# Two-layer diffusion transformer block on one core: modulation sums of the second layer begun two steps sooner, and the last gate multiplied into weights instead of results

## The chip, the cores and the metric

The kernel runs as one launch on one core of a Trainium2 chip. A core has five engines with queues of their own: PE (TensorE, matmuls), DVE (VectorE), ACT (ScalarE), POOL (GpSimd) and SP (SyncE, which here only issues DMAs). Every instruction waits in its engine's queue behind the one ahead of it. The metric is the time of one execution in device microseconds (us), the median of several runs.

## The reference

Two layers over 256 latent tokens and 256 context tokens of width 1024. Each layer modulates its input, mixes (layer 0: retention, layer 1: neighbourhood attention), adds the result through a gate, normalizes, modulates again, runs an MLP of width 4096 and adds that through a second gate. Only the latent rows of layer 1 are returned. What matters here:

```python
def sq_relu_mlp(h, w1, w2):
    return jnp.square(jax.nn.relu(h @ w1)) @ w2
...
    for i in range(DEPTH):
        mod = (silu_c @ ada_w[i] + ada_b[i])[:, None, :]
        mod_c = silu_cc @ ada_w[i] + ada_b[i]
        sh1, sc1, g1, sh2, sc2, g2 = jnp.split(mod, 6, axis=-1)
        ...
        x = layer_norm(DN_ALPHA * x + g1 * y, ln_g[i, 0], ln_b[i, 0])
        h = x * (1.0 + sc2) + sh2
        x = layer_norm(DN_ALPHA * x + g2 * sq_relu_mlp(h, mlp_w1[i], mlp_w2[i]), ln_g[i, 1], ln_b[i, 1])
```

`g2` is one row of 1024 numbers, the same for all tokens, so `g2 * (hidden @ w2)` equals `hidden @ (w2 * g2)`, column by column.

## The kernel before

**Weights.** Every weight is used as a sum of two halves in a rounded 32-bit format, `hi` and `lo`, and each product takes three matmuls (hi*hi, hi*lo, lo*hi). Weights come in *units* of 512 KB: SP loads one into a buffer `raw` (pool `rawp`, four buffers), ACT casts it to `hi`, DVE subtracts to get `lo`, and that subtraction sets the `raw` buffer free. `hi` and `lo` have five buffers each (`WB = 5`), which PE sets free when it is done with a unit. The list `specs` holds the order of the units, `fetch` loads and splits one, `take` hands out the next and keeps five ahead.

**Background stream.** The modulation rows of both layers (`silu(c) @ ada_w`) are not made on PE: `bg_stream` runs in 89 small steps beside other work. A step takes a 512 KB tile `rawa` of `ada_w` (from the same four `rawp` buffers, loaded one step ahead), and DVE weighs it into `acc` (`weigh`: one pass of 128x1024 for latent alone, two passes where the context's modulation is wanted as well). After eight steps `folded` reduces `acc` to `red`; small operations on POOL (columns) or DVE and POOL (`ada_gate`) then finish a row. Steps 1 to 41 are done in the retention stage, and the other 48 belong to layer 1. A call `bg()` does one step, up to `bg_max`.

**First MLP (layer 0, 512 tokens).** The hidden width goes in two halves (`hf`). For each, eight groups `fp` of 256 hidden columns are made (two units, 48 matmuls each), then two output halves, eight units each (24 matmuls per unit). In the very last output half the last four units are *held* and used token tile by token tile, so that the next layer's start overlaps. Before the change the 48 steps run from the output halves of `hf` 0 on: one per unit there (16), then `bg(2 + fp % 2)` in the groups of `hf` 1 (20), one per unit in the third output half (8) and in the first four units of the last (4). Instructions are placed by a scheduler except where an engine is set to program order (`.on = True`); SP is always in program order.

**Second MLP (layer 1, 256 tokens) and the end.** `mm2b(t, half, u, un)` adds unit `u` (16 units of 256 hidden rows by 512 columns, for each `half`) into `parts[t, half]` for the token tile `t`. Units 0 to 12 are used as they come; units 13 to 15 of both halves (`HELD = 13`) are held and used in the order: tile 0 half 0, tile 0 half 1, tile 1 half 0, tile 1 half 1 (this last in two column quarters, in two banks of their own). `settle` multiplies a bank by the gate row `G2` and adds it to the residual rows `R`; `settle_quarter` does it for a quarter; `stat` takes the statistics of the norm, and `last_norm` and the stores end the kernel.

Names in the rows: `p` are the matmul banks, `raw` weights, `rawa` tiles of `ada_w`, `hid` the hidden activations, `r` their relu, `st` statistics, `G` a gate row. Line 84 is the helper through which all operations are issued, so nearly every row has it. The four held units of the first MLP's last output half are called h1 to h4 below; the unit ahead of them U4.

Of the kernel before, what the change touches and what calls it, by code (L numbers as in the profile page):

```python
# [17 lines left out]
P = 128  # L18
# [86 lines left out]
def kernel(  # L105
# [23 lines left out]
    pe, act, dve, pool, sp = (  # L129
        InOrder(tc, getattr(nc, e), e in PIN)  # L130
        for e in ("tensor", "scalar", "vector", "gpsimd", "sync")
    )
# [23 lines left out]
    def bank(s="ps"):  # L156
        return psp.tile([P, 512], F32, tag="ps", name=nm(s))
# [5 lines left out]
    def scr(s, dt=F32):  # L163
        return scp.tile([P, 512], dt, tag="scr", name=nm(s))
# [18 lines left out]
    specs = []  # L183
# [54 lines left out]
    def spec_w2(u, half):  # L238
        w_rows(mlp_w2[1], u * 256, 256, half * 512, 512)


    scratch_units = set()
    for u in range(16):
        for half in range(2):
            if (u, half) == (10, 0):
                scratch_units.add(len(specs))
                spec_w2(13, 0)
            if (u, half) != (13, 0):
                spec_w2(u, half)

    units = []
# [3 lines left out]
    def fetch(n, in_scratch=False, at=None):  # L255

        for src, k, ncol in specs[len(units) : len(units) + max(n, 0)]:
            raw = rawp.tile([P, k, ncol], F32, tag="raw", name=nm("raw"))
            sp.dma_start(out=raw[:], in_=src.rearrange("(k p) n -> p k n", p=P))
            if in_scratch or len(units) in scratch_units:  # L260
                hi, lo = Rows([scr("hi", F32R) for _ in range(k)]), Rows([scr("lo", F32R) for _ in range(k)])
                for i in range(k):
                    act.copy(out=hi[:, i, :], in_=raw[:, i, :])
                    pending.append((lo[:, i, :], raw[:, i, :], hi[:, i, :]))
                units.append((hi, lo))
                continue
            if at is None:
                hi = hip.tile([P, k, ncol], F32R, tag="hi", name=nm("hi"))
                lo = lop.tile([P, k, ncol], F32R, tag="lo", name=nm("lo"))
            else:  # L270
                both = slot(at, [P, 2, k, ncol], F32R, "hilo")
                hi, lo = both[:, 0], both[:, 1]
            act.copy(out=hi[:], in_=raw[:])
            pending.append((lo[:], raw[:], hi[:]))
            units.append((hi, lo))
# [99 lines left out]
    R = [RR[t // 2][:, t % 2, :] for t in range(4)]  # L375
# [180 lines left out]
    def bg(n=1):  # L556
        for _ in range(n):
            if bg_done[0] < bg_max[0]:
                flush()
                bg_done[0] += 1  # L560
                next(bgs, None)
# [5 lines left out]
    def load_gate(l, w, nt=2, eng=nc.scalar):  # L567
        G = cpool.tile([P, 2, D], F32, tag="G", name=nm("G"))
        gt = grow[l, w]
        for t in range(nt):  # L570
            eng.dma_start(out=G[:, t, :], in_=gt[t : t + 1, :].broadcast_to([P, D]))
        return G
# [83 lines left out]
    def stat(t, half):  # L656
        if half == 0:
            stats[t] = smp.tile([P, 2, 6], F32, tag="st", name=nm("st"))
        dve.bn_stats(out=stats[t][:, half, :], in_=R[t][:, half * 512 : (half + 1) * 512])
# [212 lines left out]
    def part_v(k, a, b):  # L872
# [8 lines left out]
        out=lgn[:, 0], in_=ret_decay[0].rearrange("(o d) h -> o (d h)", o=1).broadcast_to([P, 8])  # L881
# [118 lines left out]
    for h in range(RH):  # L1000
# [9 lines left out]
        else:  # L1010
# [15 lines left out]
            for u in range(4):  # L1026
                ((wh, wl),) = take(1)
                for t in range(4):
                    for kk in range(2):
                        k = 2 * u + kk  # L1030
# [72 lines left out]
        for t in range(4):  # L1103
            po = bank("po")
            scs = list(range(4)) if t < 2 else [2, 3]
            for i, sc in enumerate(scs):
# [9 lines left out]
                out=on, in0=po[:], scalar1=mv[:, 0:1], scalar2=r[:], op0=ALU.subtract, op1=ALU.mult  # L1116
# [51 lines left out]
        else:  # L1168
# [35 lines left out]
            tmp = proj(1, 1)  # L1204
# [10 lines left out]
            tmp = proj(2, 1)  # L1215
# [54 lines left out]

    G2 = None
    for hf in range(2):
# [46 lines left out]
        for fp in range(len(hid), 8):  # L1319
            ht = hslot(fp)  # L1320
            pb = [bank("p1") for _ in range(2)]
            us = take(2)
            mm1(us, ALL, pb)
            pe.on = False
            dve.on = hf == 0
            evac1(pb, ALL, ht)
            if hf == 0 and fp < 6:
                residual(fp - 2, xns[fp - 2], gb, dve)
            dve.on = False
            hid.append(ht)  # L1330
            if hf:
                bg(2 + fp % 2)
            if hf == 0 and fp < 6:
                for q in range(16 * (fp - 2), 16 * (fp - 1)):
                    shifted_biases(q)
        if G2 is None:
            G2 = load_gate(0, 1)
        for half in range(2):
# [19 lines left out]
            if not last:  # L1358
                for t in range(4):
                    accumulate(pb[t], t, half, G2)  # L1360
                continue
            bg_until(89)
            held = take(4)
# [14 lines left out]
            def settle(t):  # L1378

                add_to(t, 1, gated(pb[t], t, 1, G2), dve)  # L1380
                stat(t, 1)
                return moments(t)
# [336 lines left out]
    p2 = turn(2)  # L1719
# [183 lines left out]
    ps = bank("pnw")  # L1903
# [93 lines left out]
    ps = [wo_last(1, 1, cols) for cols in HALVES]  # L1997
# [58 lines left out]


    G2 = load_gate(1, 1, 1)
    HS1 = [N_Q, N_V, N_B, N_P0, N_P1, N_OH, N_OL, N_K1]
    hid = [ht]  # L2060
    for f4 in range(1, 8):
# [22 lines left out]

    FULL = slice(0, 512)
    parts = {(t, half): [(bank("p2"), FULL)] for t in range(2) for half in range(2)}
    HELD = 13

    def mm2b(t, half, u, un, only=None):
        wh, wl = un  # L2090
        for i, (ps, cols) in enumerate(parts[t, half]):
            if only in (None, i):
                for kk in range(2):
                    k = 2 * u + kk
                    ht = hid[k // 4]
                    mm3(
                        ps[:, cols],
                        (ht[:, k % 4, 0, tsl(t)], ht[:, k % 4, 1, tsl(t)]),
                        (wh[:, kk, cols], wl[:, kk, cols]),
                        k == 0 or (len(parts[t, half]) > 1 and k == 2 * HELD),  # L2100
                        k == 31 or (t == half == 1 and k == 2 * HELD - 1),
                    )

    held = {}
    for u in range(HELD):
        if u == 10:
# [13 lines left out]
    def quarter(q):  # L2120
        return slice(256 * q, 256 * q + 256)
# [3 lines left out]

    def settle_quarter(q):
        ps = parts[1, q // 2][q % 2][0][:, quarter(q % 2)]
        tmp = scr("acc")
        dve.tensor_mul(out=tmp[:, :256], in0=ps, in1=G2[:, 0, quarter(q)])
        dve.tensor_add(out=R[1][:, quarter(q)], in0=R[1][:, quarter(q)], in1=tmp[:, :256])  # L2130
        stat_quarter(q)

    def stat_quarter(q):
# [14 lines left out]
        if a:  # L2148
            (sp, act)[half].dma_start(out=out[0, tsl(t), sl], in_=xn)

    for half in range(2):
        for u in range(13, 16):
            mm2b(0, half, u, held[u, half])
        if half == 0:
            settle(1, 1)
            parts[1, 1] = [(bank("p2"), slice(256 * q, 256 * q + 256)) for q in range(2)]
        settle(0, half)
        stat(0, half)
    m0 = moments(0)
    for half in range(2):  # L2160
        last_norm(0, 0, half, *m0)
# [51 lines left out]
```

## Time and profile before

| | |
|---|---|
| median of 3 runs | 1175.99 us (1175.35 to 1176.32) |
| the profiled execution | 1176.32 us, span of its instructions 1174.4 us |
| granted TensorE clock | 0.998 of full speed |
| busy: PE, DVE, ACT, POOL | 1161.8, 848.4, 481.1, 235.1 us |
| instructions | 17544 |
| HBM read, written | 189.12 MB, 5.75 MB |

Matmul records overlap each other (a 128x512 matmul is shown with 0.39 us, while the next one starts 0.23 us later), so PE's pace is read from the distance of starts and its waits from larger distances. An `[idle <-X]` at the end of a row is the time that this engine stood idle ahead of the row, and what ended it. A row with xN merges N like operations.

### The profile page before, as it was taken

The page shows a single profiled execution, that of the slowest core. Times are in us where ns is not written, and L with a number is a line of the kernel's source. Part 1 is how long each engine was busy: PE and PEld are TensorE (multiplying, and loading weights), DVE is VectorE, ACT ScalarE, POOL GpSimd, SP SyncE. Part 2 cuts the span into 40 slices and gives each one's busy share as a digit, 9 for nine tenths or more (in the row PEclk, how much of TensorE's full clock was granted, in tenths as well). Part 3 has the DMA queues.
Part 4 walks back from the last instruction along what each step waited for, and adds up shares of the span by engine and source line. Part 5 has one row for each costly group of instructions (what it writes and reads, how often), then busy time and mean ns, then how long its engine had stood idle before and what let it go on. Part 6 is the DMA issues. An engine that isn't in the chain of part 4 may idle for free.

```text
span 1174.4 us, 17544 instructions
## 1 busy us (share of the span) xinstructions
PE 1161.8 (99%) x6687; PEld 980.7 (84%) x6687; DVE 848.4 (72%) x1361; ACT 481.1 (41%) x819; POOL 235.1 (20%) x418
## 2 busy tenths in 40 slices
PE   9999999999999999999999999999999999999997
PEld 6788888888888889888888888879778878999886
DVE  3786687777898787757777675578577589877456
ACT  3643332222323246441212333137466666756341
POOL 0102001010220241770312001223443430000001
PEclk9999999999999999999999999999999999999999
DMA  9943552544355426756556665646344335766760
GB/s 275 277 130 105 162 187 96 156 153 144 112 178 177 140 65 220 181 113 215 177 184 198 211 200 179 197 157 202 81 136 144 107 113 160 214 206 205 237 215 36
DMA packets 140115, 195.10 MB, mean 166 GB/s; under 512 B 9936, under 2 KB 81136, under 8 KB 140032
## 3 DMA queue, kind: packets, MB, share of 16 engines
q1 hardware_dynamic: 131904, 182.03, 49.8%
q0 software_dynamic: 6976, 9.39, 3.8%
q10 hardware_dynamic: 1152, 2.56, 0.7%
q8 instruction: 52, 0.85, 0.3%
q14 instruction: 31, 0.25, 0.1%
HBM read 189.12 MB, written 5.75 MB: 166 GB/s over the span
## 4 chain that ended last, share of the span: by engine, by line
PE 74%; DMA 12%; DVE 8%; issue 3%; ACT 2%; POOL 0%; DVEq 0%; ACTq 0%
PE p L84 23%; DMA rawa<-in_ada_w_dram 11%; PE pq L84 8%; PE pv L84 8%; PE pw L84 7%; PE pg L84 7%; PE pn L84 4%; DVE acc L84 4%; PE pnv L84 4%; PE po L84 3%; DVE lo L84 3%; PE pnw L84 1%; PE ppt L84 1%; PE pS L84 1%; PE pav L84 1%
## 5 line engine op out<-in xcount | busy, mean ns | idle before, releaser
L84 ACT CAST hi<-raw 128x1024 fp32r<-128x1024 f32 (+2 forms) x228 | 231.9, 1032 | 306.7 <-PE p L84 114.2
L84 DVE TENSOR_TENSOR lo<-raw,hi 128x1024 fp32r<-128x1024 f32 (+2 forms) x228 | 272.6, 1210 | 101.3 <-ACT hi L84 101.1
L84 PE MATMUL p<-hi,hid 128*128 128x512 f32 (+1 forms) x780 | 238.2, 386 | 0.0
L84 PEld LDWEIGHTS p<-hi,hid 128*128 128x128 f32 x780 | 145.7, 188 | 29.3
L84 PE MATMUL p<-hTl,hi 128*128 128x256 f32 (+1 forms) x512 | 165.9, 326 | 0.0
L84 PE MATMUL p<-hTh,lo 128*128 128x256 f32 (+1 forms) x512 | 165.9, 326 | 0.0
L84 PE MATMUL p<-hTh,hi 128*128 128x256 f32 (+1 forms) x512 | 162.6, 327 | 0.0
L84 PE MATMUL p<-lo,hid 128*128 128x512 f32 (+1 forms) x390 | 150.8, 387 | 2.1 <-DVE lo L84 2.1
L84 DVE SCALAR_TENSOR_TENSOR acc<-rawa,scol,acc 128x1024 f32<-128x1024 f32 x56 | 74.4, 1341 | 65.1 <-DMA rawa<-in_ada_w_dram 65.1
L84 PEld LDWEIGHTS p<-hTh,lo 128*128 128x128 f32 x512 | 96.3, 188 | 8.8
L84 PEld LDWEIGHTS p<-hTl,hi 128*128 128x128 f32 x512 | 96.4, 188 | 8.7
L84 PEld LDWEIGHTS p<-hTh,hi 128*128 128x128 f32 x512 | 94.3, 188 | 8.7
L84 PEld LDWEIGHTS p<-lo,hid 128*128 128x128 f32 x390 | 73.3, 188 | 17.9 <-DVE lo L84 3.2
L84 DVE SCALAR_TENSOR_TENSOR strips<-rawa,scol,strips 128x512 f32<-128x512 f32 x112 | 78.6, 764 | 0.0
L84 ACT CAST hid<-r 128x256 fp32r<-128x256 f32 (+1 forms) x64 | 31.9, 500 | 112.4 <-DVE r L84 112.3
L84 POOL TENSOR_TENSOR rstd<-rstd,misc 128x1 f32<-128x1 f32 x28 | 19.1, 684 | 216.5 <-DVE rstd L84 215.5
L84 ACT ACTIVATE s<-s,mn 128x512 f32<-128x512 f32 x64 | 45.5, 713 | 21.6 <-DVE mn L84 21.6
L84 PE MATMUL pw<-hi,oh 128*128 128x512 f32 x128 | 50.8, 397 | 0.0
L84 PE MATMUL pg<-hi,hTh 128*128 128x512 f32 x128 | 50.6, 395 | 0.0
L84 PE MATMUL pw<-hi,ol 128*128 128x512 f32 x128 | 50.0, 390 | 0.0
L84 PE MATMUL pg<-hi,hTl 128*128 128x512 f32 x128 | 49.9, 390 | 0.0
L84 PE MATMUL pw<-lo,oh 128*128 128x512 f32 x128 | 49.8, 389 | 0.0
(241 smaller groups left out, 2275.2 us busy)
## 6 DMA issues: line engine op xcount, KB each, us to landing
raw<-in_mlp_w_dram SPq DMA_DIRECT2D x128, 512.0 KB, 4.5
rawa<-in_ada_w_dram SPq DMA_DIRECT2D x80, 512.0 KB, 3.9
raw<-in_ret_w_in_dram SPq DMA_DIRECT2D x42, 512.0 KB, 4.0
raw<-in_nat_w_in_dram SPq DMA_DIRECT2D x24, 512.0 KB, 4.1
rawq<-in_ada_w_dram SPq DMA_DIRECT2D x16, 512.0 KB, 6.0
raw<-in_ret_w_o_dram SPq DMA_DIRECT2D x16, 512.0 KB, 3.5
bias<-rpb_rows POOLq DMA_DIRECT2D x32, 128.0 KB, 2.9
raw<-in_nat_w_o_dram SPq DMA_DIRECT2D x8, 512.0 KB, 3.7
```

What stands on the lines that cost most here:

```text
L84: r = f(*args, **kwargs)
```

## The change

Three things are changed.

1. In the groups `fp` 6 and 7 of the first MLP's first half, one `bg()` each is added. The 48 steps of layer 1 so begin two calls sooner and end two calls sooner; the last two calls, in the units ahead of the held ones, find nothing left to do.
2. The units (13, 1), (14, 1) and (15, 1) of the second MLP's second half are multiplied in place by the gate row on DVE, after their load and before their split.
3. For half 1, the banks of units 0 to 12 are closed at unit 12 for both token tiles (before: only tile 1) and settled through the gate; units 13 to 15 go to new banks, which are added to `R` without a gate.

```diff
+    HELD = 13
+    scratch_units, scaled_units, scale_row = set(), set(), [None]
     for u in range(16):
         for half in range(2):
             ...
             if (u, half) != (13, 0):
+                if half == 1 and u >= HELD:
+                    scaled_units.add(len(specs))
                 spec_w2(u, half)
...
             sp.dma_start(out=raw[:], in_=src.rearrange("(k p) n -> p k n", p=P))
+            if len(units) in scaled_units:
+                dve.tensor_mul(
+                    out=raw[:], in0=raw[:], in1=scale_row[0].unsqueeze(1).broadcast_to([P, k, ncol])
+                )
...
             if hf:
                 bg(2 + fp % 2)
+            elif fp > 5:
+                bg()
...
     G2 = load_gate(1, 1, 1)
+    scale_row[0] = G2[:, 0, 512:1024]
...
-                        k == 0 or (len(parts[t, half]) > 1 and k == 2 * HELD),
-                        k == 31 or (t == half == 1 and k == 2 * HELD - 1),
+                        k == 0 or (half == 1 and k == 2 * HELD),
+                        k == 31 or (half == 1 and k == 2 * HELD - 1),
...
     def settle_quarter(q):
         ps = parts[1, q // 2][q % 2][0][:, quarter(q % 2)]
-        tmp = scr("acc")
-        dve.tensor_mul(out=tmp[:, :256], in0=ps, in1=G2[:, 0, quarter(q)])
-        dve.tensor_add(out=R[1][:, quarter(q)], in0=R[1][:, quarter(q)], in1=tmp[:, :256])
+        dve.tensor_add(out=R[1][:, quarter(q)], in0=R[1][:, quarter(q)], in1=ps)
         stat_quarter(q)
...
-    for half in range(2):
-        for u in range(13, 16):
-            mm2b(0, half, u, held[u, half])
-        if half == 0:
-            settle(1, 1)
-            parts[1, 1] = [(bank("p2"), slice(256 * q, 256 * q + 256)) for q in range(2)]
-        settle(0, half)
-        stat(0, half)
+    for u in range(HELD, 16):
+        mm2b(0, 0, u, held[u, 0])
+    settle(0, 0)
+    stat(0, 0)
+    for t in range(2):
+        settle(t, 1)
+    parts[0, 1] = [(bank("p2"), FULL)]
+    parts[1, 1] = [(bank("p2"), slice(256 * q, 256 * q + 256)) for q in range(2)]
+    for u in range(HELD, 16):
+        mm2b(0, 1, u, held[u, 1])
+    dve.tensor_add(out=R[0][:, FULL.stop :], in0=R[0][:, FULL.stop :], in1=parts[0, 1][0][0][:])
+    stat(0, 1)
```

How instructions move, at three places. First, SP's queue around group `fp` 6 of the first half, before:

```order
L84 DMA raw_4560<-in_mlp_w_dram 128x2x512
L84 DMA raw_4627<-in_mlp_w_dram 128x2x512
L84 DMA raw_4633<-in_mlp_w_dram 128x2x512
L84 DMA raw_4704<-in_mlp_w_dram 128x2x512
L84 DMA raw_4710<-in_mlp_w_dram 128x2x512
L84 DMA rawa_4740<-in_ada_w_dram 128x2x512
L84 DMA raw_4746<-in_mlp_w_dram 128x2x512
L84 DMA rawa_4776<-in_ada_w_dram 128x2x512
L84 DMA raw_4780<-in_mlp_w_dram 128x2x512
```

and with the change:

```order
L84 DMA raw_4560<-in_mlp_w_dram 128x2x512
L84 DMA rawa_4624<-in_ada_w_dram 128x2x512
L84 DMA raw_4633<-in_mlp_w_dram 128x2x512
L84 DMA raw_4639<-in_mlp_w_dram 128x2x512
L84 DMA rawa_4703<-in_ada_w_dram 128x2x512
L84 DMA raw_4714<-in_mlp_w_dram 128x2x512
L84 DMA raw_4720<-in_mlp_w_dram 128x2x512
L84 DMA rawa_4750<-in_ada_w_dram 128x2x512
L84 DMA raw_4754<-in_mlp_w_dram 128x2x512
L84 DMA rawa_4784<-in_ada_w_dram 128x2x512
```

The four weight units that stood ahead of the first of these `rawa` tiles (4627 to 4710) now have two of them (4624, 4703) in between; from there on each weight unit stands behind two more `rawa` tiles than before, until the stream ends. The very first tile of the stream (step 0, `rawa_3389`) is loaded long ahead in both.

Second, DVE's queue at the end of the stream. Before, from step 46's weighing to the second held unit (h1's subtraction writes `lo_6281`, h2's `lo_6314`; `p_929` and `p_930` are banks of the third output half):

```order
L84 SCALAR_TENSOR_TENSOR acc_6161<-rawa_6341,scol,acc_6161 128x1024
L84 TENSOR_TENSOR acc_6268<-p_929_5977,G_4697 128x512
L84 BN_STATS st_6420<-R_104 128x6
L84 TENSOR_TENSOR acc_6271<-p_930_5978,G_4697 128x512
L84 TENSOR_TENSOR lo_6281<-raw_6278,hi_6280 128x1024
L84 BN_STATS st_6422<-R_104 128x6
L84 SCALAR_TENSOR_TENSOR acc_6161<-rawa_6374,scol,acc_6161 128x1024
L84 BN_STATS st_6424<-R_105 128x6
L84 TENSOR_REDUCE red_6160<-acc_6161 128x32
L84 BN_STATS st_6426<-R_105 128x6
L84 COPY gate_6452<-red_6160 64x32
L84 TENSOR_TENSOR lo_6314<-raw_6311,hi_6313 128x1024
```

With the change, from the last step's weighing (h1 is `lo_6287`; behind the last row stand six small gate operations and then `lo_6320`, h2):

```order
L84 SCALAR_TENSOR_TENSOR acc_6101<-rawa_6314,scol,acc_6101 128x1024
L84 TENSOR_REDUCE red_6100<-acc_6101 128x32
L84 TENSOR_TENSOR lo_6238<-raw_6235,hi_6237 128x1024
L84 TENSOR_TENSOR acc_6268<-p_929_5981,G_4707 128x512
L84 TENSOR_TENSOR acc_6271<-p_930_5982,G_4707 128x512
L84 BN_STATS st_6420<-R_104 128x6
L84 TENSOR_TENSOR acc_6274<-p_931_5983,G_4707 128x512
L84 BN_STATS st_6422<-R_104 128x6
L84 BN_STATS st_6424<-R_105 128x6
L84 TENSOR_TENSOR acc_6277<-p_932_5984,G_4707 128x512
L84 TENSOR_TENSOR lo_6287<-raw_6284,hi_6286 128x1024
L84 BN_STATS st_6426<-R_105 128x6
```

The last weighing and its reduction now stand ahead of U4 (`lo_6238`) and of all four settled banks, and no weighing is left between h1 and the others.

Third, DVE's queue over the second MLP's last units. Before, from unit (11, 1) on ((12, 0), (12, 1), (13, 1), (14, 0), (14, 1), (15, 0), (15, 1)):

```order
L84 TENSOR_TENSOR lo_10778<-raw_10775,hi_10777 128x1024
L84 TENSOR_TENSOR lo_10784<-raw_10781,hi_10783 128x1024
L84 TENSOR_TENSOR lo_10802<-raw_10799,hi_10801 128x1024
L84 TENSOR_TENSOR lo_10820<-raw_10817,hi_10819 128x1024
L84 TENSOR_TENSOR lo_10838<-raw_10835,hi_10837 128x1024
L84 TENSOR_TENSOR lo_10856<-raw_10853,hi_10855 128x1024
L84 TENSOR_TENSOR lo_10874<-raw_10871,hi_10873 128x1024
L84 TENSOR_TENSOR lo_10892<-raw_10889,hi_10891 128x1024
```

and with the change:

```order
L84 TENSOR_TENSOR lo_10778<-raw_10775,hi_10777 128x1024
L84 TENSOR_TENSOR raw_10817<-raw_10817,G_9373 128x1024
L84 TENSOR_TENSOR lo_10784<-raw_10781,hi_10783 128x1024
L84 TENSOR_TENSOR lo_10802<-raw_10799,hi_10801 128x1024
L84 TENSOR_TENSOR raw_10854<-raw_10854,G_9373 128x1024
L84 TENSOR_TENSOR lo_10821<-raw_10817,hi_10820 128x1024
L84 TENSOR_TENSOR lo_10839<-raw_10836,hi_10838 128x1024
L84 TENSOR_TENSOR raw_10891<-raw_10891,G_9373 128x1024
L84 TENSOR_TENSOR lo_10858<-raw_10854,hi_10857 128x1024
L84 TENSOR_TENSOR lo_10876<-raw_10873,hi_10875 128x1024
L84 TENSOR_TENSOR lo_10895<-raw_10891,hi_10894 128x1024
```

Each of the three multiplications stands two subtractions ahead of its own unit's, and so in front of subtractions of units that are already loaded. The order of PE's matmuls and of SP's loads is unchanged here.

More of the change, by code (lines that the diff above doesn't have):

```diff
@@ L239, in spec_w2 @@
         w_rows(mlp_w2[1], u * 256, 256, half * 512, 512)
-    scratch_units = set()
+    HELD = 13
+    scratch_units, scaled_units, scale_row = set(), set(), [None]
     for u in range(16):
@@ L2086 @@
     parts = {(t, half): [(bank("p2"), FULL)] for t in range(2) for half in range(2)}
-    HELD = 13
     def mm2b(t, half, u, un, only=None):
```

## The prediction, on record before the changed kernel ran

> **What bounds the kernel now.** I read the page's busy shares first, then the waits, then PE's timeline at the only place where PE waits, then the chain of work through that place.
>
> ```profile
> PE 1161.8 (99%) x6687; PEld 980.7 (84%) x6687; DVE 848.4 (72%) x1361; ACT 481.1 (41%) x819; POOL 235.1 (20%) x418
> PE p L84 <- DVE lo L84: 2.1, 2, 1.7
> ```
>
> PE is busy for 99% of the span, but a modelled matmul overlaps the next one, so the share alone proves little. The second row, from the waits between 760 and 775 us, is the better witness: PE waited there for DVE's `lo` of a weight unit, twice, and its timeline shows what that cost.
>
> ```profile
> 765.02 0.39 PE L84 MATMUL p<-lo,hid 128*128 128x512 f32 x1
> 765.70 0.39 PE L84 MATMUL p<-lo,hid 128*128 128x512 f32 x1
> 768.23 0.50 PE L84 MATMUL p<-lo,hid 128*128 128x512 f32 x1 [1.70 <-DVE lo L84]
> 770.33 0.50 PE L84 MATMUL p<-lo,hid 128*128 128x512 f32 x1 [0.43 <-DVE lo L84]
> 772.52 0.39 PE L84 MATMUL p<-lo,hid 128*128 128x512 f32 x1
> ```
>
> Matmuls with `lo` come once in three, 0.68 us apart at full pace (765.02 to 765.70). Between 765.70 and 772.52 there are six such distances, 4.08 us at pace, and they took 6.82: PE lost **2.74 us** at the held units h1 to h4. Behind the first 60 us I found no other distance of starts far beyond the pace, so nearly everything that is to be gained lies here or behind PE's last matmul. The chain of waits through this place:
>
> ```profile
> 748.30 3.97 DMA rawa<-in_ada_w_dram
> 753.68 3.59 DMA rawa<-in_ada_w_dram
> 759.11 3.90 DMA rawa<-in_ada_w_dram
> 763.10 1.28 DVE acc L84
> 764.91 1.23 DVE red L84
> 766.95 1.23 DVE lo L84
> 769.07 1.22 DVE lo L84
> ```
>
> It is the background stream in lock step: a tile lands after some 3.6 to 4.0 us, DVE weighs it, a buffer comes free, the next tile is asked for. One turn takes about 5.3 us. The weight units' `lo` stand between these in DVE's queue and come as late as the stream does. The three tiles shown are those of steps 45, 46 and 47, the last; 763.10 is step 47's weighing.
>
> **The two steps that begin sooner.** They are two turns of the same lock step, taken out of its end and put into groups 6 and 7 of the first half. There:
>
> ```profile
> 511.75 1.05 ACT L84 CAST hi<-raw 128x1024 fp32r<-128x1024 f32 x1 [0.22 <-PE p L84]
> 515.56 1.23 DVE L84 TENSOR_TENSOR lo<-raw,hi 128x1024 fp32r<-128x1024 f32 x1 [1.50 <-ACT hi L84]
> 518.07 0.69 DVE L84 TENSOR_TENSOR hid<-r,hid 128x512 fp32r<-128x512 f32 x1 [0.69 <-ACT hid L84]
> 522.63 1.05 ACT L84 CAST hi<-raw 128x1024 fp32r<-128x1024 f32 x1 [0.56 <-PE p L84]
> 528.18 1.41 DVE L84 TENSOR_SCALAR acc<-rawa,scol 128x1024 f32<-128x1024 f32 x2
> 530.11 2.47 DVE L84 SCALAR_TENSOR_TENSOR acc<-rawa,scol,acc 128x1024 f32<-128x1024 f32 x2
> 538.85 1.22 DVE L84 TENSOR_TENSOR lo<-raw,hi 128x1024 fp32r<-128x1024 f32 x1
> ```
>
> The casts of weights wait for PE here, that is for a free `hi` buffer: weights run as far ahead as buffers allow, and DVE has gaps. Step 0 (1.41 us, at 528.18) can follow the `hid` operation that ends at 518.76, step 1 (2.47) comes right behind, then step 2, whose tile takes the place in SP's queue that the change gives it. So 1.41 + 2 x 2.47 = 6.4 us of DVE work lands in gaps before 527.5, where before nothing of the stream had run. Until step 0 is weighed two of the four `raw` buffers hold stream tiles, and SP passes two more of them ahead of each weight unit. The third weight unit is then asked for when the `lo` of 515.56 sets a buffer free, at 516.8; with the slowest load quoted below, 5.2 us, it lands at 522.0, before its cast can start at 522.63, and that cast waits for PE. So this costs nothing, and what hides it is the lead of the weights. Following buffers and DVE's order on, I get the `lo` of 538.85 at about 538.4 with step 5 behind it instead of step 3. The stream is then two steps and 0.45 us ahead; six units later, by the same count, two steps and 3 us.
>
> At the end step 47 stands where step 45 stood: its weighing is over at about 753.6 (748.30 + 3.97 + 1.28), if the stream has no further lead. What follows is DVE's own work:
>
> ```profile
> 754.70 1.28 DVE L84 TENSOR_TENSOR acc<-p,G 128x512 f32<-128x512 f32 x2
> 755.47 2.54 POOL L84 TENSOR_TENSOR R<-R,acc 128x512 f32<-128x512 f32 x2 [26.43 <-DVE acc L84]
> 759.61 0.68 DVE L84 BATCH_NORM_STATS2 st<-R 128x6 f32<-128x512 f32 x1
> 759.77 3.53 POOL L84 TENSOR_TENSOR R<-R,acc 128x512 f32<-128x512 f32 x2 [1.76 <-DVE acc L84]
> 760.80 1.35 DVE L84 TENSOR_TENSOR lo<-raw,hi 128x1024 fp32r<-128x1024 f32 x1
> ```
>
> Reduction 1.23 and U4's `lo` 1.22: 756.0. Four settled banks at 0.64 and three statistics at 0.68, which wait for POOL's additions at 1.27 each: 761.7. h1's `lo`: 763.0. The fourth statistic and six small gate operations (five of these took 768.18 to 769.07 above, 0.18 each): 764.8. Then h2, h3, h4 at 1.2: 766.0, 767.2, 768.4. PE at pace wants h1's `lo` at 765.02 and the others 1.36 us apart (two triples of 0.68): 766.38, 767.74, 769.10. All four are met, by 2.0, 0.4, 0.5 and 0.7 us with no lead at all and by up to 3 us more with it. Bounds of this term: 0 (the lead is lost on the way) to 2.74 us gained; I take **2.74**, since even without the lead the count closes. Work behind it (the first settled tile, the next layer's start) hangs on PE's own matmuls and moves with them.
>
> **The gate in the weights.** Three multiplications of 128x1024 with both inputs in SBUF: 3 x 1.22 us by the like-shaped `lo` rows. DVE has 1.5 us of idle time in each 2.72 us unit here, but they stand in the queue ahead of other units' `lo` and wait for loads.
>
> ```profile
> 1129.67 1.23 DVE L84 TENSOR_TENSOR lo<-raw,hi 128x1024 fp32r<-128x1024 f32 x1 [1.50 <-ACT hi L84]
> raw<-in_mlp_w_dram SPq DMA_DIRECT2D x17, 512.0 KB, 4.5
> raw<-in_mlp_w_dram SPq DMA_DIRECT2D x1, 512.0 KB, 5.2
> raw<-in_mlp_w_dram SPq DMA_DIRECT2D x1, 512.0 KB, 3.4
> 1150.37 0.39 PE L84 MATMUL p<-lo,hid 128*128 128x512 f32 x1
> ```
>
> The chain: (13, 1) is asked for at 1130.9, when the first row's `lo` frees a buffer; it lands 4.5 us later (median; 5.2 and 3.4 are the slowest and quickest single loads seen at this end, the quick one with no other under way). Multiplication and the `lo` of (12, 0) take 2.4; that frees the buffer for (14, 1): 4.3 more, then 2.4 for its multiplication and the `lo` of (13, 1); that frees the buffer for (15, 1), which loads alone, 3.4; its multiplication, the `lo` of (14, 1) and of (15, 0) take 3.6. Sum: 1130.9 + 4.5 + 2.4 + 4.3 + 2.4 + 3.4 + 3.6 = 1151.5. PE wants (15, 0) two units behind 1150.37: 1153.09. Cover 1.6 us; cost **0**. With 5.2 for each load it is 1154.9, a stall of 1.8 us; that is the other end. (15, 1), wanted at 1157.2, has more room.
>
> Behind the matmuls:
>
> ```profile
> 1158.50 0.69 DVE L84 TENSOR_TENSOR acc<-p,G 128x512 f32<-128x512 f32 x1 [1.93 <-PE p L84]
> 1162.98 3.00 POOL L84 TENSOR_TENSOR xn<-xn,gb 128x512 f32<-128x512 f32 x2 [0.83 <-ACT xn L84]
> 1163.31 1.52 DVE L84 TENSOR_TENSOR R<-R,acc 128x512 f32<-128x512 f32 x1
> 1166.58 0.28 PE L84 MATMUL p<-hi,hid 128*128 128x256 f32 x1
> 1166.89 0.42 DVE L84 TENSOR_TENSOR acc<-p,G 128x256 f32<-128x256 f32 x1
> 1167.35 0.42 DVE L84 TENSOR_TENSOR R<-R,acc 128x256 f32<-128x256 f32 x1
> 1167.81 0.43 DVE L84 BATCH_NORM_STATS2 st<-R 128x6 f32<-128x256 f32 x1
> ```
>
> The last quarter starts at 1166.89, right behind PE's end at 1166.86, and needs two operations ahead of its statistics. With the change it needs one: **0.46 us** off the end (1167.35 to 1166.89). The four settle operations for half 1's first banks (4 x 0.73) now fill the 1.93 us gap ahead of 1158.50 and run over it; tile 0's addition then starts near 1159.5 and, one operation shorter, its statistics end 0.3 us later than before. That moves POOL's additions of 1162.98 by 0.3, and with them the 1.52 us addition, to about 1165.1; two statistics and the third quarter (0.75 + 0.46 + 0.46) end at 1166.8, just under 1166.89. Bounds of this term: 0 to 0.46.
>
> **Sum.** The profiled execution took 1176.32 us (the slowest of the three, 0.33 above the median; its span is 1174.4). 1176.32 - 2.74 - 0.46 = 1173.1; against the median, **1172.8**. A measurement of this kernel can tell about 0.2%, 2.35 us, from no change.
>
> **Rivals.**
>
> *The held units stay late.* The addition at 1163.31 took 1.52 us beside POOL, the same form 0.69 alone; at 760.80 the `lo` beside POOL took 1.35 instead of 1.22, and POOL's pair 3.53 instead of 2.54. In the new order h1's `lo` comes straight behind the last settled bank, when POOL adds it. By the rows that is 0.13 to 0.83 us on a `lo`, and h2 has 0.4 to spare with no lead: PE loses up to about 0.4, and up to 1.5 if h1 and its neighbours are hit more than once: 1173.2 to 1174.3. [...]
>
> *The tail stalls.* With loads of 5 us and more in the chain to (15, 0), PE stalls for up to 1.8 us: 1173.0 to 1174.6, or up to 0.46 more if the third quarter, 0.1 us ahead of PE's end by the count, is late as well. It decides from the point where the three loads sum to over 13.8 us.
>
> *Slower.* The units in the middle of the stream have nearly nothing to spare:
>
> ```profile
> 714.64 2.35 DVE L84 TENSOR_TENSOR lo<-raw,hi 128x1024 fp32r<-128x1024 f32 x2
> 715.96 0.44 PE L84 MATMUL p<-lo,hid 128*128 128x512 f32 x1
> ```
>
> The first of these `lo` ends 0.1 us before PE uses it. Each unit now stands behind two more stream tiles, about 2 x 5.3 us. What was hidden before 527 must cover that; each microsecond that it does not beyond 0.1 stalls PE at 690 to 716. Slower by 0.2% needs 3.2 + 2.35 + 0.1 = 5.7 us uncovered, half of the two steps, and gives 1178.4 or more. My count says that it is covered with 0.45 to 3 us over.
>
> *The first part does nothing:* the lead is used up in the middle without a stall there and the four `lo` come as late as before. Then 0.46 is left: 1175.5.
>
> **Chances.** Both parts work as counted 0.60 (own range 1172.2 to 1173.6); held units late 0.17; tail 0.08; nothing from the first part 0.08; slower 0.07. Faster by over 0.2% (under 1173.6): the first and about half of the second and a third of the third, 0.71; within: 0.22; slower 0.07. The range of 1171.7 to 1175.4 takes in the first three cases, with the spread of the runs below.
>
> **What would show it.** PE's waits for `lo` between 760 and 775 gone, distances of 0.68 through the held units; the first weighing of the second layer near 519; h1's `lo` near 762 or sooner; no idle PE near 690 to 716 nor at 1153; three multiplications `raw<-raw,G`; one operation between PE's last matmul and the last statistics. A PE wait for `lo` at any of these places would make the prediction wrong.

## The result and the profile after

| | before | after |
|---|---|---|
| median, first measurement (14 runs each) | 1175.82 us | 1173.12 us (1172.25 to 1177.11) |
| median, on another chip (29 and 12 runs) | 1175.14 us | 1173.00 us |
| profiled execution | 1176.32 us, span 1174.4 | 1173.14 us, span 1171.0 |

The ratio of the first measurement is 0.9978, with an interval of 0.9969 to 0.9988; of the second 0.9982 (0.9966 to 0.9997). The medians differ by 2.7 and 2.1 us, about 0.2%: faster, as both intervals lie below 1, but near the smallest difference that can be told here. The forecast was 1172.8 us.

The share of each engine in the chain that ended last, from the page, first of before and then of after:

```profile
PE 74%; DMA 12%; DVE 8%; issue 3%; ACT 2%; POOL 0%; DVEq 0%; ACTq 0%
PE 94%; DVE 2%; DMA 1%; ACT 1%; issue 1%; POOL 0%; ACTq 0%; DVEq 0%; SPq 0%
```

PE's share of busy time stays at 99%, and so it says nothing here; the chain does. Before, 20% of it ran through DMA and DVE, most of that through the tiles of the stream and their weighings (the page gives 11% to the loads of `rawa` and 4% to `acc`). After, nearly all of it is PE: behind the kernel's opening PE hardly waits any more. PE's timeline through the held units, of after:

```profile
764.87 0.39 PE L84 MATMUL p<-lo,hid 128*128 128x512 f32 x1
...
766.23 0.39 PE L84 MATMUL p<-lo,hid 128*128 128x512 f32 x1
...
768.95 0.39 PE L84 MATMUL p<-lo,hid 128*128 128x512 f32 x1
```

Six triples from 764.87 to 768.95 take 4.08 us, 0.68 each: no wait, where before six of them took 6.82. DVE's timeline ahead of it, of after:

```profile
748.65 1.29 DVE L84 SCALAR_TENSOR_TENSOR acc<-rawa,scol,acc 128x1024 f32<-128x1024 f32 x1 [2.98 <-DMA rawa<-in_ada_w_dram]
...
758.29 1.22 DVE L84 TENSOR_TENSOR lo<-raw,hi 128x1024 fp32r<-128x1024 f32 x1
...
762.60 4.61 DVE L84 TENSOR_TENSOR lo<-raw,hi 128x1024 fp32r<-128x1024 f32 x4
758.45 2.20 POOL L84 TENSOR_TENSOR R<-R,acc 128x512 f32<-128x512 f32 x1 [1.40 <-DVE acc L84]
```

The stream's last weighing starts at 748.65 instead of 763.10, h1's `lo` at 758.29 instead of 760.80, and h2's at 762.60 (the first of the four merged in that row) instead of 766.95. h2's is done near 763.8, and PE wants it at 766.23, 2.4 us later. The last row is POOL's addition beside h1's `lo`. The end, of after (DVE's multiplications and the `lo` behind the third, PE's use of unit (15,0), then PE's last matmul and the two DVE operations behind it):

```profile
1132.83 1.23 DVE L84 TENSOR_TENSOR raw<-raw,G 128x1024 f32<-128x1024 f32 x1 [2.08 <-DMA raw<-in_mlp_w_dram]
1139.19 1.23 DVE L84 TENSOR_TENSOR raw<-raw,G 128x1024 f32<-128x1024 f32 x1 [2.87 <-DMA raw<-in_mlp_w_dram]
1146.08 1.23 DVE L84 TENSOR_TENSOR raw<-raw,G 128x1024 f32<-128x1024 f32 x1 [3.39 <-DMA raw<-in_mlp_w_dram]
1147.23 3.49 DVE L84 TENSOR_TENSOR lo<-raw,hi 128x1024 fp32r<-128x1024 f32 x3
1150.22 0.39 PE L84 MATMUL p<-lo,hid 128*128 128x512 f32 x1
1163.70 0.28 PE L84 MATMUL p<-hi,hid 128*128 128x256 f32 x1
1164.02 0.42 DVE L84 TENSOR_TENSOR R<-R,p 128x256 f32<-128x256 f32 x1 [0.60 <-PE p L84]
1164.48 0.43 DVE L84 BATCH_NORM_STATS2 st<-R 128x6 f32<-128x256 f32 x1
```

All three multiplications wait for their loads. The second of the three `lo` is that of (15,0): it ends near 1149.6, and PE uses it at 1150.22, so 0.64 us were left. From the start of PE's last matmul to that of the last statistics it is 0.78 us; before it was 1.23 (1166.58 to 1167.81).

### The profile page after: what moved, and what is told of

It reads as the page before. It is cut to its first block, busy times and chain, and to the rows that moved or that the text cites. A ratio compares the mean times of both kernels' runs of the same rounds, so it can differ in the third digit from the quotient of the medians.

```text
span 1171.0 us, 17545 instructions
## 1 busy us (share of the span) xinstructions
PE 1160.9 (99%) x6687; PEld 980.6 (84%) x6687; DVE 850.3 (73%) x1363; ACT 480.8 (41%) x819; POOL 232.5 (20%) x418
## 4 chain that ended last, share of the span: by engine, by line
PE 94%; DVE 2%; DMA 1%; ACT 1%; issue 1%; POOL 0%; ACTq 0%; DVEq 0%; SPq 0%
PE p L84 44%; PE pq L84 8%; PE pv L84 8%; PE pw L84 7%; PE pg L84 7%; PE pn L84 5%; PE pnv L84 4%; PE po L84 2%; PE ppt L84 2%; PE pnw L84 1%; PE pS L84 1%; PE pav L84 1%; PE pqk L84 1%; PE pt L84 1%; PE pada L84 1%; PE p1t L84 1%
```

## The experiments

Times of one kernel are spread over some microseconds from run to run, so medians are set beside those of the kernel before from the same measurement, and where PE lost time is read from each run's profile. The loss at a place is the sum of distances of starts there, less what the same matmuls take at pace.

**The first part alone.**

```diff
             if hf:
                 bg(2 + fp % 2)
+            elif fp > 5:
+                bg()
```

> Only the two background steps begin sooner; the gate stays out of the weights. Theory (the whole 2.74 us of PE's waiting at the held units h1 to h4 came from the stream's last two turns): 2.7 us less than the kernel before, ratio 0.9977, and the end of the kernel as before, with two DVE operations between PE's last matmul and the last statistics. Rival (a good part of the gain is the second MLP's new order): 1.4 us or less, ratio 0.9988 or higher.

Measured: 1173.34 us against 1175.28, ratio 0.9989 (0.9977 to 1.0). The profile has no PE wait for `lo` at the held units (h2's is there 2.7 us ahead of its use), span 1171.3. The medians differ by 1.9 us, between theory and rival; the ratio is on the rival's side (0.9988 or higher), and its interval reaches from the theory to no change. So the times alone don't decide. The profile does: the wait is gone with this part alone.

**The second part alone.** The rest of the diff without the lines above.

> Only the gate goes into the last weights; the background stream stands as in the kernel before. Theory: PE still waits 2.7 us at the held units, and the end gains one 128x256 operation, 0.46 us: ratio 0.9996. Rival one (the three multiplications cost PE something that the whole change hides): no change or slower, ratio 1.0000 to 1.0010, with a PE wait for lo near 1152. Rival two (the end gains more than one operation): 1.4 us, ratio 0.9988.

Measured: 1175.23 us against 1175.28, ratio 0.9997 (0.9983 to 1.0012), span 1173.4. Its profile shows the old wait, and the new end:

```profile
767.79 0.50 PE L84 MATMUL p<-lo,hid 128*128 128x512 f32 x1 [1.02 <-DVE lo L84]
769.88 0.50 PE L84 MATMUL p<-lo,hid 128*128 128x512 f32 x1 [0.42 <-DVE lo L84]
1166.02 0.28 PE L84 MATMUL p<-hi,hid 128*128 128x256 f32 x1
1166.34 0.42 DVE L84 TENSOR_TENSOR R<-R,p 128x256 f32<-128x256 f32 x1 [0.61 <-PE p L84]
1166.80 0.43 DVE L84 BATCH_NORM_STATS2 st<-R 128x6 f32<-128x256 f32 x1
```

0.78 us from the last matmul to the last statistics again, 0.45 less than before. So the second part gives 0.45 us at the end in the profile, and too little for the times to tell. The loss at the held units was 2.05 us here (five triples in 5.45 us instead of 3.40), not 2.74.

**The kernel before once more.**

> A second profile of the kernel before. Theory (the waiting at the held units is there in every run): again 2 to 3 us between 765 and 775, by the distances of the lo matmuls. Rival (the stream's timing varies between runs, so that the wait is at times small; its fastest single runs of 1172.5 us say so): less than 1 us, and the time of that run is below 1174.

Measured: 1177.04 us, a single run. At the held units, from its profile:

```profile
765.15 0.39 PE L84 MATMUL p<-lo,hid 128*128 128x512 f32 x1
...
766.41 0.50 PE L84 MATMUL p<-lo,hid 128*128 128x512 f32 x1 [0.42 <-DVE lo L84]
...
768.51 0.51 PE L84 MATMUL p<-lo,hid 128*128 128x512 f32 x1 [0.43 <-DVE lo L84]
...
769.98 0.39 PE L84 MATMUL p<-lo,hid 128*128 128x512 f32 x1
```

Five triples in 4.83 us: 1.43 lost. Neither expectation holds as it stands: the wait is there, but its size changes from run to run, 2.74, 2.05 and 1.43 in the three profiles that have the stream at its old place. The profile that the prediction was made from was one with much to gain. The quickest single runs of this kernel, 1172.3 and 1172.5 us, are as quick as the quickest of the changed one (1172.25), so some executions probably lose next to nothing here; none of them was profiled.

**One step sooner.**

```diff
+            elif fp > 6:
+                bg()
```

> The stream begins one step sooner instead of two, gate not in the weights. Theory (lock step: one step is one turn of 5.3 us at the end, more than the 2.74 us that were lost): step 47's weighing ends near 758.6 or sooner, h2's lo near 766.8 with no further lead, where 766.38 is wanted, so 2.3 to 2.7 us gained, ratio 0.9977 to 0.9980. Rival (gain in proportion to the steps): 1.4 us, ratio 0.9988, with a PE wait of 1.4 us left.

Measured: 1173.69 us against 1175.28, ratio 0.9997 (0.9986 to 1.0008); its runs fall in two groups, six from 1172.7 to 1173.7 and five from 1175.4 to 1176.0. By the ratio that is no gain clear of noise. The profile (one of the second group, 1175.98) has no wait at the held units: first the `lo` of h2 to h4, then PE's first use of h2.

```profile
761.14 3.48 DVE L84 TENSOR_TENSOR lo<-raw,hi 128x1024 fp32r<-128x1024 f32 x3
766.25 0.39 PE L84 MATMUL p<-lo,hid 128*128 128x512 f32 x1
```

One step removes the whole loss, with 3.9 us to spare at h2. The changed kernel had 2.4 in its first profile and 3.7 in a second, so the two are not told apart. What made this execution long lies elsewhere (last section).

**One step later, two steps later.** The first unit, or the first two, of the first output half make no step; the steps left over are made ahead of the held units.

```diff
                 for t in range(4):
                     mm2(t, u, un)
-                bg()
+                if hf or half or u:        # two later: u > 1
+                    bg()
```

> The stream begins one step later than in the kernel before (no step in the first unit of the first output half); the last step is then made ahead of the held units' take, and its weighing stands behind h2's subtraction. Theory (lock step of 5.3 us a turn): step 47 is weighed near 769.7, its reduction and the gate operations end near 771.8, h3's lo near 773.0 where 767.74 is wanted at pace: PE loses 5.3 us instead of 2.74, so 2.5 us slower than before, ratio 1.0021. Rival one (the stream can catch up over its 48 steps, and the wait at the end comes from the order of DVE's queue alone): no change, ratio 0.9995 to 1.0005. Rival two (each step costs its full turn on PE): 5.3 us slower, ratio 1.0045.

> The stream begins two steps later than in the kernel before (none in the first two units of the first output half). Steps 46 and 47 are weighed behind h2, ahead of h3. Theory (each step later holds h3 back by a part of a turn, and a PE wait of over some 4 us is followed by a stretch of matmuls at half pace): a wait of 5 to 8 us at h3, then about 5 us at 0.43 us a matmul, as behind the 4.43 us wait with one step later; 1181 to 1186 us. For the slow stretch: if it is a fixed time, it is again 5.1 us; if it grows with the wait, it is longer.

Measured, one later: 1182.11 us against 1175.28, ratio 1.0063 (1.0043 to 1.0083). PE at h3, and the window of 10 us around it (PE, PE weight loads, DVE, ACT, POOL busy, then PE's granted clock):

```profile
767.32 0.61 PE L84 MATMUL p<-hi,hid 128*128 128x512 f32 x2
772.37 0.80 PE L84 MATMUL p<-lo,hid 128*128 128x512 f32 x1 [4.43 <-DVE lo L84]
772.96 1.05 PE L84 MATMUL p<-hi,hid 128*128 128x512 f32 x2
...
777.46 0.40 PE L84 MATMUL p<-lo,hid 128*128 128x512 f32 x1
770.00:780.00 10.00, 7.63 (x24) 6.09 (x25) 6.84 (x14) 1.04 (x1) 0.51 (x1) 0.66 0.95 288
```

h3's `lo` ended at 772.3, counted near 773.0, and PE lost 4.6 us there and 0.7 near 691. Then came a cost that no theory had: for 5.1 us, from 772.37 to 777.46, PE ran at 0.43 us a matmul, at a granted clock of 0.66 over the window, and lost 2.4 us more (12 matmuls in 5.09 us instead of 2.72). Together 7.7 us, 5.0 more than in the profile of before; the spans differ by 4.2.

Measured, two later: 1174.64 us against 1175.33, ratio 0.9998 (0.9982 to 1.0015), and the profiled execution, the quickest of the eight, took 1172.72, span 1170.9. The expectation failed altogether: in this execution there was no wait and no slow stretch. DVE through the end of the stream, and PE's use of h4:

```profile
751.75 1.34 DVE L84 TENSOR_TENSOR lo<-raw,hi 128x1024 fp32r<-128x1024 f32 x1
...
756.46 1.20 DVE L84 TENSOR_TENSOR lo<-raw,hi 128x1024 fp32r<-128x1024 f32 x1
...
761.69 1.28 DVE L84 SCALAR_TENSOR_TENSOR acc<-rawa,scol,acc 128x1024 f32<-128x1024 f32 x1 [1.20 <-DMA rawa<-in_ada_w_dram]
762.89 1.22 DVE L84 TENSOR_TENSOR lo<-raw,hi 128x1024 fp32r<-128x1024 f32 x1
...
766.49 2.34 DVE L84 TENSOR_TENSOR lo<-raw,hi 128x1024 fp32r<-128x1024 f32 x2
768.34 0.39 PE L84 MATMUL p<-lo,hid 128*128 128x512 f32 x1
```

The stream began two steps later than in the kernel before, and its last weighing (761.69) still came no later than there (763.10, and 762.66 and 761.15 in the two other profiles with the stream at its old place). h1 and h2 are split at 751.75 and 756.46, 9.1 and 10.5 us sooner than before, and h4 is ready 0.65 us ahead of PE. Being late by one step is thus worse than being late by two.

**Three and six steps sooner.**

```diff
+            elif fp > 5:
+                bg(fp - 5)                 # six: bg(3)
```

> Three steps sooner (one in group 6, two in group 7 of the first half), gate not in the weights. Theory (nothing more to gain at the held units; the more steps stand in front, the nearer the middle of the stream comes to waiting, as with six steps, which waited 1.2 us at 681 to 693): no wait at the held units, distances of the lo at 690 to 716 between those of two steps (3 to 5 us) and of six (0.05 to 0.2 us), time as the first part alone, 1173.3 us, or up to 1 us more. Rival (three steps gain more): under 1172.5 us.

> The stream begins six steps sooner (three in each of the groups 6 and 7 of the first half), gate not in the weights. Theory (only the 2.74 us of waiting at the held units can be gained, and one step was enough for it): no more than the first part alone, 1173.3 us, with h1's lo not later than 757.75, and no stall where the six steps begin, as weights run five buffers ahead of PE there. Rival one (the cover of the start is used up: each weight unit stands behind six tiles more, four turns of 5.3 us more than with two steps): PE waits for lo between 520 and 720, slower than the first part alone by the uncovered part, up to 10 us or more. Rival two (a longer lead gains more): under 1172.5 us.

Measured, three: 1174.44 us against 1175.33, ratio 0.9996 (0.9983 to 1.0009); no wait at the held units, but some 0.2 us near 716, where the `lo` ended 0.05 us ahead of PE. Measured, six: 1178.19 us against 1175.14, ratio 1.0017 (1.0001 to 1.0033). Where the steps begin nothing waits, the least distance there being 3.9 us; the waits come in the middle, in the second half's groups:

```profile
681.04 0.39 PE L84 MATMUL p<-hTl,hi 128*128 128x512 f32 x1
682.11 0.50 PE L84 MATMUL p<-hTh,lo 128*128 128x512 f32 x1 [0.68 <-DVE lo L84]
...
692.94 0.39 PE L84 MATMUL p<-hTl,hi 128*128 128x512 f32 x1
693.48 0.50 PE L84 MATMUL p<-hTh,lo 128*128 128x512 f32 x1 [0.15 <-DVE lo L84]
```

0.84 and 0.31 us in a profiled execution that was among the quickest of this kernel (1175.45); what the slower ones lost, which make the median, no profile shows. The places are near those that the rival "slower" had named (690 to 716), and the cover at the start was not what failed. Set side by side, by steps sooner, from the profile of the run named above for each (for 0 from three: before, the second part alone, before once more; for 2 from the first part alone):

| steps | last weighing starts at | least distance of `lo` to PE, 640 to 720 | PE lost at held units | median (before, same measurement) |
|---|---|---|---|---|
| -2 | 761.7 | 6.7 us | 0 | 1174.6 (1175.3) |
| -1 | 767.3 | 0.05 | 4.6, and 2.4 slow | 1182.1 (1175.3) |
| 0 | 763.1, 762.7, 761.2 | 0.1, 0.5, 1.9 | 2.74, 2.05, 1.43 | - |
| 1 | 752.6 | 3.9 | 0 | 1173.7 (1175.3) |
| 2 | 748.1 | 3.3 | 0 | 1173.3 (1175.3) |
| 3 | 747.1 | 0.05 | 0 | 1174.4 (1175.3) |
| 6 | 732.9 | 0.05 | 0 (1.15 in the middle) | 1178.2 (1175.1) |

One profile is one sample here too: the four other profiles with two steps (the changed kernel twice, and with more multiplications at its end) have the last weighing at 745.9 to 749.0 and least distances of 1.7 to 4.8 us. So one step and two are not told apart by these columns.

**Each multiplication twice, four times.**

```diff
-            if len(units) in scaled_units:
+            for _ in range(2 * (len(units) in scaled_units)):   # or 4
```

> Whole change, but each of the three multiplications by the gate is made twice (the last three units are so multiplied by the gate's square; the result differs in that). Theory (multiplications and loads form one chain to unit (15,0), with 0.64 us of cover in the changed kernel's profile): the chain grows by 3 x 1.23 = 3.69 us, PE waits 3.0 us ahead of (15,0), and the time is that of the whole change plus 3.0, 1176 us; up to 2.5 us more if PE runs slowly behind that wait, as it did behind the 4.43 us wait of the run with one step later (0.43 us a matmul instead of 0.23 for 5.1 us). Rival (the loads alone set the chain, the multiplications lie in DVE's gaps): no PE wait, 1173.1 us.

> Whole change, but each of the three multiplications is made four times (the last units so carry the gate's fourth power). Counted along DVE's queue from the load of (13,1): only one multiplication of each unit stands between its load and the freeing of the buffer that the next load waits for; of the others, two of (14,1) and two of (15,1) and the next ones stand ahead of the lo of (15,0). With loads of 4.3, 3.7 and 3.6 us the lo of (15,0) ends 23.4 us behind the asking for (13,1); PE wants it 22.2 us behind it. Theory (this chain sets the lo of (15,0)): PE waits 1.2 us there (0.5 to 2.5 by the loads), 1174.2 us, no slow PE behind so short a wait. Rival (PE is not held by this chain at all, as the run with two multiplications could be read): no wait, 1173.1 us.

Measured, twice: 1173.19 us against 1173.00 for the whole change on the same chip. No PE wait. The first theory fell, by a fault of its count. From DVE's timeline, the load of (13,1) to the `lo` of (15,0):

```profile
1131.46 1.23 DVE L84 TENSOR_TENSOR raw<-raw,G 128x1024 f32<-128x1024 f32 x1 [1.48 <-DMA raw<-in_mlp_w_dram]
1132.61 1.22 DVE L84 TENSOR_TENSOR lo<-raw,hi 128x1024 fp32r<-128x1024 f32 x1
1133.74 1.22 DVE L84 TENSOR_TENSOR raw<-raw,G 128x1024 f32<-128x1024 f32 x1
...
1145.83 1.22 DVE L84 TENSOR_TENSOR raw<-raw,G 128x1024 f32<-128x1024 f32 x1
1146.96 2.51 DVE L84 TENSOR_TENSOR lo<-raw,hi 128x1024 fp32r<-128x1024 f32 x2
```

The second multiplication of (13,1) (1133.74) stands behind the `lo` (1132.61) that frees the buffer for the next load, and so beside that load; only the one at 1145.83 lengthens the chain. Between the asking for (13,1) and the end of (15,0)'s `lo` it was 20.9 us here, 21.5 and 19.7 in two profiles of the whole change; PE wants it at 22.2. The three loads took 11.2, 13.0 and 11.1 us. Less its loads, the chain is 9.7 us with doubled multiplications and 8.6 without: one multiplication more, not three.

Measured, four times: 1177.49 us (1176.36 to 1183.97), ratio 1.0021 (1.0004 to 1.0039), 4.5 us above the whole change's 1173.00 of the other measurement.

```profile
1150.48 0.49 PE L84 MATMUL p<-hi,hid 128*128 128x512 f32 x1 [0.49 <-ACT hi L84]
1151.93 0.50 PE L84 MATMUL p<-lo,hid 128*128 128x512 f32 x1 [0.96 <-DVE lo L84]
1156.74 0.50 PE L84 MATMUL p<-lo,hid 128*128 128x512 f32 x1 [0.40 <-DVE lo L84]
1166.30 0.28 PE L84 MATMUL p<-hi,hid 128*128 128x256 f32 x1
1168.81 0.43 DVE L84 BATCH_NORM_STATS2 st<-R 128x6 f32<-128x256 f32 x1
```

The corrected chain holds: PE waits for (15,0)'s `lo`, 1.2 us by the distance of starts. What the count had not seen is around it: 0.65 us for (15,0)'s `hi`, which ACT casts behind that of (14,1), and 0.6 us for (15,1). Behind PE's last matmul it is 2.51 us to the last statistics instead of 0.78, as the settling of half 1's first banks stood behind these multiplications on DVE. So PE can be made to stall at the tail, as a rival of the prediction had it for slow loads; with one and two multiplications a unit no profile shows it.

**The whole change again, and one step sooner with the gate in the weights.**

> The whole change once more, on the same chip as the next runs. Theory (the first part gains the 2.7 us of waiting at the held units, the second 0.46 us at the end): 0.4 us below the first part alone (1173.34 us by its median), so about 1172.9, and no PE wait for lo. Rival (the multiplications cost what the shorter end gains): 1173.3 or more.

> One step sooner instead of two, with the gate in the last weights. Theory (the wait at the held units is all that the stream's start can give, and one step removes it): the time of the whole change, 1173.0 us, with no PE wait for lo and h2's lo 2.5 us or more ahead of PE. Rival one (one step leaves a wait in some runs): 1173.5 or more in the median. Rival two (the larger distances of the one-step version are worth something): 1172.5 or less.

Measured: 1173.00 us and 1172.80 us, ratios 0.9982 (0.9966 to 0.9997) and 0.9987 (0.9973 to 1.0001), no PE wait for `lo` in either, h2 ready 3.7 and 4.3 us ahead. The two can't be told apart in time, and no version here is clearly quicker than the changed kernel.

## Why the prediction was right, point by point

**Where the time was lost.** Right. The 2.74 us at the held units went, PE stands 2.9 us earlier by 1150 (1150.37 to 1147.50 for the same matmul), and behind the opening no PE wait for `lo` is left. That the loss was read from one execution is the limit: in two others it was 2.05 and 1.43, so the median gained 2.1 to 2.7 us for both parts where the sum had 3.2.

**The start of the stream costs nothing.** Right. Step 0's weighing came where it was forecast, in the gap behind the `hid` operation; the row is of after.

```profile
518.63 1.41 DVE L84 TENSOR_SCALAR acc<-rawa,scol 128x1024 f32<-128x1024 f32 x2
516.76 0.37 SPq L84 DMA_DIRECT2D raw<-in_mlp_w_dram  x1
```

The second row is the asking for the third weight unit: 516.76, counted 516.8. Even six steps found cover there. In the middle, where the rival *slower* had PE stall, the `lo` of 715.9 was 3.2 us ahead of PE after the change, where it had been 0.1.

**Two turns taken out of the end.** The size was about right and the reason was not. The last weighing moved by 14.45 us, two turns of 5.3 and 3.9 us of further lead, of which up to 3 had been counted. But the two turns are not what brings it: one step brought it forward by 8.5 to 10.5 us (752.6 against 761.2 to 763.1), and two steps *later*, which by the lock step should have cost 10.6 us, left it where it had been. A turn has no fixed price, and that two was a good number was in part luck: one step the other way lost PE 4.6 us at the held units. The step count also changes how the stream's tiles and their weighings (two passes in steps 0 to 15, one from step 16 on) fall among DVE's other work. One reading of it is DVE's waiting for tiles around the passage to the second half, from the waits between 595 and 638 us: first before, then two steps later (total, times, longest).

```profile
DVE acc L84 <- DMA rawa<-in_ada_w_dram: 15.3, 8, 3.9
DVE acc L84 <- DMA rawa<-in_ada_w_dram: 9.1, 6, 2.5
```

Two later, the last two-pass steps and their row's end lie in that passage. DVE waits 6.2 us less there, and 4.4 less than in the second profile of the kernel before (13.5). From about 656 to 716 the `lo` of a unit then stands some 5 to 7 us further ahead of PE than in the first profile of before, and some 2 to 5 further than in the second. That the one brings the other is not shown: for one step sooner the same total is 15.9, and its lead comes from elsewhere. From about 648 to 692 the distance of each group's second unit shrinks in all versions, by 1.2 to 4.4 us, so the lead at the start of these groups matters for the places near 691 and 716. Why it comes out as it does for each step count stays open; no version changed it by itself.

The held units are another matter, and there the prediction's count (all four are met even with no lead) was borne out. Three steps sooner had 0.05 us left at 716, no more than the kernel before, and yet lost nothing at the held units, with h2's `lo` 3.3 us ahead of PE. In that version the last weighing (747.05) stands ahead of U4's `lo` (750.71); in the kernel before it stands between h1 and h2.

**DVE's work behind the stream.** Right, with more room than counted: h1's `lo` starts at 758.29 and not at 761.7, h2's ends near 763.8 and not at 766.0. The fourth statistic of `R` waited 1.2 us for POOL, which hid in that room.

**The held units stay late (rival).** Did not happen. POOL's addition of 758.45 ran beside h1's `lo` and took 2.20 us, 1.27 alone; the `lo` took 1.22, as alone. So POOL lost 0.9 us and DVE nothing. The `lo` had started 0.16 us earlier, and from its end at 759.5 POOL needed 1.15 us, about its usual time. In the pair at 1163.31 of the kernel before, which gave the rival its 0.83 us, POOL's operation had begun first, 0.33 us ahead (1162.98): it took 1.30 us, and DVE's addition 1.52 instead of 0.69. In both pairs the one begun first kept its time and the other lost; that it is always so, two pairs do not show.

**The tail.** The chain was followed rightly, and its cost was 0. The cover was mis-sized in this execution: 0.64 us instead of 1.6, as the lone last load took 4.4 us (asked for when the `lo` of (13,1) ended, landed ahead of 1146.08) where 3.4 had been taken from the quickest row; in the second profile it took 3.4, and the cover was 2.5. The end gained 0.45 of the 0.46 us. The third quarter had 0.6 us to spare where 0.1 had been counted.

## What to carry to other kernels

Where loads, splits and background tiles share one ring of buffers and one engine's queue, the price of moving a step isn't a turn of the ring: look at which of the operations behind it PE will wait for, and try the neighbours on both sides, since here one place later was worse than two. A wait seen in one profile is one sample; take a second profile of the kernel before, before counting it in full. A multiplication moved into weights lengthens the chain of loads where it stands between a load and the freeing of the buffer that the next load waits for, and not where it runs beside a load; here one of each unit stood there and was hidden, with 0.64 and 2.5 us to spare in two profiles.

## What the hardware showed that was not expected

Behind a PE wait of 4.43 us the matmuls ran at 0.43 us each instead of 0.23 for 5.1 us. The granted clock was 1.00 from 760 to 770, 0.66 from 770 to 780 and 1.00 again from 780 to 790. PE's last matmul ahead of the wait had ended at 767.9, so the clock fell about 2 us into the wait or later. From 777.46 on the matmuls were at pace again. If the clock was low only until then, its mean from 770 on was about 0.54, an estimate from the 0.66 (3.4 us of full clock missing in 7.46); the pace, 0.23 us to 0.43, fell to 0.53. Of the nine runs of this kernel eight had a mean granted clock of 0.995 to 0.997 and took 1179.2 to 1185.7 us; the ninth, at 0.999, took 1174.76. Behind PE waits of 1.7 us and less the profiles show no such stretch: the granted clock is 1.00 from 760 to 780 in the kernel before, and from 1140 to 1165 with four multiplications. So this wait cost 2.4 us on top of its 4.6, in the one profile that has it. That the wait brought the fall is my reading of it; how long a wait must be for that, between 1.7 and 4.43 us, no run here shows.

Two of fourteen profiles, one of the kernel before and the one with one step sooner, had a slower stretch from about 1010 to 1080, in the second MLP's 256-column products, without any wait and with a granted clock of 1.00: each matmul started 0.118 us behind the one before instead of 0.113. The first row is of the run with one step sooner, the second of the first part alone: 87 matmuls in 10 us against 90.

```profile
1030.00:1040.00 10.00, 10.00 (x87) 10.00 (x86) 7.54 (x13) 5.52 (x12) 0.00 (x0) 1.00 0.65 193
1030.00:1040.00 10.00, 10.00 (x90) 10.00 (x90) 7.52 (x13) 5.79 (x11) 0.00 (x0) 1.00 0.66 199
```

It cost 2.6 and 2.8 us, as much as the change gains, and near the distance between the two groups of times above (2.6 us between their medians); whether it makes the upper group of the other kernels too is not shown. Its cause is open.
